# Block 1's rotary as two VectorE products and a TensorE sum, and its low weight parts kept off GpSimd

## The chip, the cores and the metric

One core of a Trainium2 chip runs the whole program in one launch. The metric is the device time of that program in microseconds (us); the kernel's figure is the median of three timed runs. Beside these there is one profiled execution, from which every row below comes. Engines carry their profile names: PE is TensorE's matmul, PEld its weight load, DVE is VectorE, ACT is ScalarE, POOL is GpSimd, SP is SyncE, which here issues most DMAs.

## The reference, cut to what matters

Two layers of a first block (gated delta rule, sparse attention with an indexer, mixture of experts) are followed by two layers of a second block. The change lies almost wholly in the first block's attention. There, five column groups of one projection are turned by rotary tables before they are used:

```python
def apply_rope(x, cos, sin):
    half = x.shape[-1] // 2
    rot = jnp.concatenate([-x[..., half:], x[..., :half]], -1)
    return x * cos + rot * sin          # per position and feature

proj = h @ w_in[l]                      # h: 272 x 1024, w_in: 1024 x 4176
q, k, qi, ki = (apply_rope(...) for the columns of sq, sk, iq, ik)
score = sum over 8 heads of relu(qi . ki / 8) * wi      # the indexer
sel   = top 64 keys of each query by score
out   = softmax(q . k / 8 over sel) @ v
```

The features lie in pairs 32 apart within each head of 64, and cos and sin are the same for both of a pair. In the second block the memory tokens are normed by rows (`rms_norm(mem, g)`) before a projection; one line of that is touched too.

## The kernel before, in words

Activations are held transposed, features on the 128 partitions and the 272 positions in the free dimension, as a high and a low part (`hh` and `hl`, L259 and L260). A weight tile of 1024 x 128 is split in the same way by `split`: ACT writes the high part `wh` (L244), and the low part `wl` (L245) is the difference, made on DVE, or on GpSimd for every fourth split, since `K.lo_pool` is 4 all through the first block. `ws` (L384) then multiplies: for each of 8 slices of 128 features three matmuls of 128x272 in the one-pass format (L252 high by high, L253 high by low, L254 low by high; the trace prints their type as f32), 24 in all, into one of three PSUM banks with the tag "d".

`rope` (L510) follows 13 such products in each of two layers: one for the indexer's keys `ikT`, four for its queries `iqT`, four for the keys `skT` and four for the queries `sqT`. It copies PSUM to `rraw` on ACT (L515, or L513 with the factor 0.125 for `sqT`), lets TensorE exchange the halves by a full float32 matmul against the constant `rot` (L517, into the single bank of tag "o"), multiplies `rraw` by cos on GpSimd (L519), the exchanged values by sin on DVE (L520), and adds both on GpSimd (L521).

The order on each engine is set at build time by a list scheduler, so a change of one engine's work moves its neighbours too. Around the first five ropes of a layer the delta rule still runs (L1151 to L1189: PE products of a state, sums on DVE, a power on GpSimd at L1178, which is followed by L1180 on DVE and the transposes L1183 on PE). Around the last eight the indexer runs: score products on PE (L543), relu on ACT (L546), weighted sums on DVE (L547), and eight rounds of maximum and replacement on DVE (L552, L553). After the ropes come the attention itself (L659 to L701), then the projection (`Project`, L252 to L254 again, with 512 columns), the norm (L788 to L865), routing, and the experts, whose weights (tiles `wb`, L1211) arrive through a ring of buffers.

`mem_kv` norms the memory rows in `memx`: a square on ACT (L1673), a power on GpSimd (L1675), and a product by a scalar for each row on DVE (L1676).

Of the kernel before, what the change touches and what calls it, by code (L numbers as in the profile page):

```python
# [8 lines left out]
F32 = mybir.dt.float32  # L9
# [4 lines left out]
OP = mybir.AluOpType  # L14
# [3 lines left out]
T1 = 272  # L18
# [355 lines left out]
def b1_attention(K, l, mix, st):  # L374
    nc, A, c = K.nc, K.A, K.c
    V, S, G, PE = nc.vector, nc.scalar, nc.gpsimd, nc.tensor
    p = K.p
    h2 = (K.hh, K.hl)
    w = A["w_in"][l]
    ident = c["ident"]  # L380
    tiles = (0, 1, 2) if l == 0 else (0, 1)

    def ws(wt, c0):
        wa = split(K, wt[:, :, c0:c0 + 128], (8, 128))  # L384
        ps = bank(K, "d")
        for k in range(8):
            mm3(K, ps[:, :T1], (wa[0][:, k], wa[1][:, k]), (h2[0][:, k, :], h2[1][:, k, :]), k == 0, k == 7)
        return ps[:, :T1]
# [118 lines left out]
    pa = K.pa = st["delta"].enter_context(K.tc.tile_pool(name="attr%d" % l, bufs=1, side="right"))  # L507


    def rope(ps, dst, scale=None):  # L510
        raw = p.tile([128, T1], F32, name="rraw", bufs=2)
        if scale:
            S.mul(raw, ps, scale)  # L513
        else:
            S.copy(raw, ps)  # L515
        pr = bank(K, "o")
        PE.matmul(pr[:, :T1], c["rot"], raw, start=True, stop=True)  # L517
        t2 = p.tile([128, T1], F32, name="rt2", tag="cva", bufs=2)
        G.tensor_tensor(dst, raw, c["cos"], op=OP.mult)  # L519
        V.tensor_tensor(t2, pr[:, :T1], c["sin"], op=OP.mult)  # L520
        G.tensor_tensor(dst, dst, t2, op=OP.add)  # L521

    K.router = router_weights(K, l, K.hp)
    ikT = p.tile([128, T1], F32, name="ikT", tag="ikT")
    rope(ws(wik.rearrange("p k a n -> p k (a n)"), 0), ikT)
# [33 lines left out]
    def heads():  # L559
        for x, o in ((skT, 2568), (sqT, 2056)):  # L560
            for b in range(2):
                wt = wcols(K, w, o + 256 * b)
                for j in range(2):

                    rope(ws(wt, j * 128), x[:, 2 * b + j, :], 0.125 if x is sqT else None)
                    yield
        for b in range(2):
            wt = wcols(K, w, 3080 + 256 * b)
            for j in range(2):
                ps = ws(wt, j * 128)  # L570
                raw = p.tile([128, T1], F32, name="rraw", bufs=2)
                S.copy(raw, ps)
                pt = bank(K)
                for t in range(3):
                    PE.transpose(pt[:TP[t], t * 128:(t + 1) * 128], raw[:, TOFF[t]:TOFF[t] + TP[t]], ident)
                ci = 2 * b + j
                for t in range(3):
                    S.copy(vtok[t][:TP[t], ci * 128:(ci + 1) * 128], pt[:TP[t], t * 128:(t + 1) * 128])
                yield
# [126 lines left out]
def router_weights(K, l, p):  # L706

    nc, A = K.nc, K.A
    V, S, G, PE = nc.vector, nc.scalar, nc.gpsimd, nc.tensor
    wr = K.pt.tile([128, 8, 36], F32, name="wr", tag="ta", bufs=2)  # L710
    nc.sync.dma_start(wr[:, :, 0:32], A["w_rtr"][l].rearrange("(k p) n -> p k n", p=128))
    nc.sync.dma_start(wr[:, :, 32:36], A["w_grp"][l].rearrange("(k p) n -> p k n", p=128))
    br = p.tile([36, 1], F32, name="br")
    nc.sync.dma_start(br[0:32], A["b_rtr"][l].rearrange("(n o) -> n o", o=1))
    nc.sync.dma_start(br[32:36], A["b_grp"][l].rearrange("(n o) -> n o", o=1))
    wrs = [p.tile([128, 8, 36], FR, name="wrs%d" % i) for i in range(2)]
    pr = bank(K, "o")
    for k in range(8):
        PE.matmul(pr[:36, 0:1], wr[:, k, :], K.lcol[:, 16 + 8 * l + k:17 + 8 * l + k], start=(k == 0), stop=(k == 7))
    with K.tc.issue_after(K.anchor.ins):  # L720
        V.tensor_tensor(br, br, pr[:36, 0:1], op=OP.add)
        V.tensor_tensor(wr, wr, K.lcol[:, 8 * l:8 * l + 8, None].to_broadcast([128, 8, 36]), op=OP.mult)
    put(K, wrs, wr, slice(None))
    return wrs, br
# [937 lines left out]
def mem_kv(K, l, pool):  # L1662

    nc, A = K.nc, K.A
    V, S, G, PE = nc.vector, nc.scalar, nc.gpsimd, nc.tensor
    mx = pool.tile([128, 2, 1024], F32, name="memx", tag="wb")
    nc.sync.dma_start(mx, A["mem_2"][0].rearrange("(t p) n -> p t n", p=128))
    yield
    mT = pool.tile([128, 8, 256], F32, name="memT", tag="wb")
    for t in range(2):  # L1670
        ss = K.pt.tile([128, 2], F32, name="rmss", bufs=2)
        sq = K.pt.tile([128, 1024], BF, name="rmsq", tag="ta", bufs=2)
        S.activation(sq, mx[:, t], AF.Square, accum_out=ss[:, 0:1])  # L1673
        V.tensor_scalar(ss[:, 0:1], ss[:, 0:1], 1.0 / 1024, 1e-6, op0=OP.mult, op1=OP.add)
        G.tensor_tensor(ss[:, 1:2], ss[:, 0:1], K.nhalf[:, 0:1], op=OP.pow)  # L1675
        V.tensor_scalar(mx[:, t], mx[:, t], ss[:, 1:2], None, op0=OP.mult)  # L1676
    g = K.lcol[:, 48 + 8 * l:56 + 8 * l]
    for b in range(4):
        ps = bank(K, "op"[b % 2])
        for kk in range(2):  # L1680
            for t in range(2):
                PE.transpose(ps[:, kk * 256 + t * 128:kk * 256 + t * 128 + 128],
                             mx[:, t, (2 * b + kk) * 128:(2 * b + kk + 1) * 128], K.c["ident"])
        V.tensor_tensor(mT[:, 2 * b:2 * b + 2, :], ps.rearrange("p (k q) -> p k q", k=2),
                        g[:, 2 * b:2 * b + 2, None].to_broadcast([128, 2, 256]), op=OP.mult)
    yield
    wv = A["mem_w_kv_2"][l].rearrange("(k p) n -> p k n", p=128)

    def proj(c0):
        ps = [bank(K, t) for t in "op"]  # L1690
        wt = []
        for b in range(2):
            wt.append(turn(K).rearrange("p (k n) -> p k n", n=512))
            nc.sync.dma_start(wt[b], wv[:, 4 * b:4 * b + 4, c0:c0 + 512])
        for b in range(2):
            for kk in range(4):
                k = 4 * b + kk
                for t in range(2):
                    PE.matmul(ps[t], mT[:, k, t * 128:(t + 1) * 128], wt[b][:, kk, :], start=(k == 0), stop=(k == 7))
            yield  # L1700
        return ps

    ps = yield from proj(0)
    if l == 1:
        m = pool.tile([128, 2048], F32, name="mkv", tag="wb")
        K.mem[1] = (m[:, 0:1024].rearrange("p (h q) -> p h q", q=256), m[:, 1024:].rearrange("p (t n) -> p t n", n=512))
    memk, memv = K.mem[l]
    kn = [mem_norm(K, x, 1.0) for x in ps]
    for t in range(2):
        S.mul(memk[:, :, t * 128:(t + 1) * 128], to_feat(K, kn[t], "op"[t]), K.lcol[:, 66 + l:67 + l])  # L1710
    yield
    ps = yield from proj(512)
    for t in range(2):
        S.copy(memv[:, t, :], ps[t])
    yield
# [638 lines left out]
```

## Time and profile before

| | |
|---|---|
| median of three runs | 2051.73 us (2047.42 to 2054.76) |
| the profiled execution, its own time | 2053.6 us |
| its span | 2051.8 us |
| PE busy | 1932.7 us, 94% of the span |
| DVE busy | 1057.3 us, 52% |
| ACT busy | 767.5 us, 37% |
| POOL busy | 353.9 us, 17% |
| GpSimd's low parts (L245) | 21 of 350, 50.4 us |
| the ropes of layer 0, of layer 1 | about 128 to 206 us, and 655 to 730 us |

A busy share is an average over stages. The rows that count are those of the two stretches in which the ropes lie; each row of a window gives the length, then for each engine the busy time and in brackets the number of instructions, then the granted share of TensorE's clock, the mean busy share of the DMA engines, and GB/s. A PE record's length holds the pipeline's depth, so back-to-back matmuls are read from start to start.

### The profile page before, as it was taken

The numbers are of one execution on the slowest core, as the hardware profiler recorded it, in microseconds if no ns is written. First come the engines' busy times: TensorE is split into PE (matmuls) and PEld (weight loads), VectorE is DVE, ScalarE is ACT, GpSimd is POOL, SyncE is SP. The second block draws the span as 40 slices with busy tenths as digits, with TensorE's granted clock in tenths as the row PEclk, the third lists the DMA queues.
The fourth block names the chain that finished last, engine by engine and source line by source line (L and its number), as shares of the span: only waits on it lengthen the run. The fifth ranks groups of instructions, "written<-read, shape, count | busy, mean of one in ns | idle before, by whom it ended". The sixth has DMA issues, their size and how long they took to land. (4 is left out here: it accounts for less than half of the span.)

```text
span 2051.8 us, 36697 instructions
## 1 busy us (share of the span) xinstructions
PE 1932.7 (94%) x15166; PEld 1523.2 (74%) x15166; DVE 1057.3 (52%) x2096; ACT 767.5 (37%) x1471; POOL 353.9 (17%) x370
## 2 busy tenths in 40 slices
PE   8999999999799998999779999999999999999999
PEld 7888755544588876544358698989888879898987
DVE  6557545222675664322165755555545675555544
ACT  4323432111341343211055344455435534445543
POOL 1325100000122620000010201224200030122410
PEclk9999989999899999999989999999999999999999
DMA  7313279999631346999973433445555353254551
GB/s 221 92 42 124 103 287 391 420 423 419 195 93 64 114 174 270 407 420 422 421 231 124 144 124 93 162 152 170 185 184 154 108 167 124 83 195 144 166 198 68
DMA packets 199341, 414.53 MB, mean 202 GB/s; under 512 B 26025, under 2 KB 147443, under 8 KB 174595
## 3 DMA queue, kind: packets, MB, share of 16 engines
q1 hardware_dynamic: 192230, 410.36, 55.1%
q10 hardware_dynamic: 6940, 1.78, 0.4%
q8 instruction: 121, 1.98, 0.4%
q14 instruction: 50, 0.40, 0.1%
HBM read 411.07 MB, written 1.05 MB: 201 GB/s over the span
## 5 line engine op out<-in xcount | busy, mean ns | idle before, releaser
L245 DVE TENSOR_TENSOR wl<-w,wh 128x1024 fp32r<-128x1024 f32 x329 | 412.9, 1257 | 263.3 <-ACT wh L244 260.0
L244 ACT CAST wh<-w 128x1024 fp32r<-128x1024 f32 x350 | 365.4, 1046 | 441.5 <-PE ps_d L253 266.5
L252 PE MATMUL ps_d<-hh,wh 128*128 128x256 f32 (+1 forms) x1632 | 485.7, 298 | 5.3 <-ACT wh L244 2.2
L254 PE MATMUL ps_d<-hh,wl 128*128 128x256 f32 (+1 forms) x1632 | 481.2, 295 | 0.2
L253 PE MATMUL ps_d<-hl,wh 128*128 128x256 f32 (+1 forms) x1632 | 478.7, 294 | 2.2 <-DVE hl L260 1.2
L252 PEld LDWEIGHTS ps_d<-hh,wh 128*128 128x128 f32 x1632 | 313.0, 192 | 17.4 <-issue 6.8
L254 PEld LDWEIGHTS ps_d<-hh,wl 128*128 128x128 f32 x1632 | 314.6, 193 | 10.3 <-DVE wl L245 6.8
L253 PEld LDWEIGHTS ps_d<-hl,wh 128*128 128x128 f32 x1632 | 313.9, 192 | 7.6 <-DVE hl L260 1.6
L1295 PE MATMUL ps_d<-wb,hg 128*32 128x256 f32 x1600 | 121.3, 388 | 6.0 <-DMA wb<-in_w 6.0
L2321 POOL TENSOR_TENSOR relu<-relu 128x256 f32<-128x256 f32 x64 | 86.7, 1354 | 130.6 <-ACT relu L2320 130.6
L1295 PEld LDWEIGHTS ps_d<-wb,hg 128*32 128x32 f32 x1600 | 59.3, 112 | 50.7 <-DMA wb<-in_w 10.5
L1327 DVE TENSOR_TENSOR yacc<-yacc,ps_c 128x512 f32<-128x512 f32 x56 | 38.5, 687 | 86.2 <-PE ps_c L1324 86.2
L1283 PE MATMUL ps_c<-oh,yp 128*128 128x128 f32 (+1 forms) x640 | 81.4, 280 | 0.0
L1283 PEld LDWEIGHTS ps_c<-oh,yp 128*128 128x128 f32 (+1 forms) x640 | 75.4, 191 | 7.9 <-issue 5.4
L1315 PE MATMUL ps_d<-wb,hid 128*32 128x512 f32 x400 | 70.5, 647 | 6.9 <-ACT hid L1309 6.8
L2275 POOL TENSOR_TENSOR mergedT<-mergedT,tg 128x256 f32<-128x256 f32 x32 | 32.6, 1040 | 239.4 <-DVE tg L2273 239.4
L245 POOL TENSOR_TENSOR wl<-w,wh 128x1024 fp32r<-128x1024 f32 x21 | 50.4, 2400 | 126.1 <-ACT wh L244 116.6
L1299 DVE SCALAR_TENSOR_TENSOR mth<-mth,ps_d 128x256 f32<-128x256 f32 x16 | 6.7, 421 | 125.2 <-ACT mth L1298 125.2
L1298 ACT ACTIVATE mth<-ps_d 128x256 f32<-128x256 f32 x16 | 6.1, 383 | 165.8 <-PE ps_d L1295 165.8
L1324 PE MATMUL ps_c<-ysl,ohT 128*128 128x512 f32 (+1 forms) x140 | 64.9, 603 | 0.0
L2322 ACT CAST hid<-relu 128x256 fp32r<-128x256 f32 x64 | 26.0, 407 | 92.3 <-POOL relu L2321 92.3
L2323 DVE TENSOR_TENSOR hid<-relu,hid 128x256 fp32r<-128x256 f32 x64 | 27.2, 425 | 58.5 <-ACT hid L2322 58.5
(697 smaller groups left out, 3578.0 us busy)
## 6 DMA issues: line engine op xcount, KB each, us to landing
wb<-in_w SPq DMA_DIRECT2D x150, 1024.0 KB, 14.3
w<-in_w_in SPq DMA_DIRECT2D x82, 1024.0 KB, 5.2
w<-in_w SPq DMA_DIRECT2D x42, 1024.0 KB, 19.6
w<-in_w_up SPq DMA_DIRECT2D x32, 1024.0 KB, 5.4
w<-in_w_down SPq DMA_DIRECT2D x32, 1024.0 KB, 5.0
w<-in_w_out SPq DMA_DIRECT2D x16, 1024.0 KB, 5.1
w<-in_w_branch SPq DMA_DIRECT2D x24, 512.0 KB, 3.6
w<-in_cmp_w SPq DMA_DIRECT2D x8, 1024.0 KB
```

What stands on the lines that cost most here:

```text
L244: K.nc.scalar.copy(h, x)
L245: eng.tensor_tensor(lo, x, h.bitcast(F32), op=OP.subtract)
L252: PE.matmul(out, a[0], b[0], start=start, stop=False, skip_group_check=True)
L253: PE.matmul(out, a[0], b[1], start=False, stop=False, skip_group_check=True)
L254: return PE.matmul(out, a[1], b[0], start=False, stop=stop, skip_group_check=True)
L1283: PE.matmul(ps[:, (k % 4) * 128:(k % 4) * 128 + 128], K.yp[t][:P, k * 128:(k + 1) * 128], oh[:P, t, :], start=(k == 4 * kk and t == ts[0] ...
L1295: PE.matmul(pu[j * 32:j * 32 + 32, i * 256:i * 256 + 256], hg[:, k, j * 32:j * 32 + 32], wts[i][j][:, k, :], start=(k == 0 and i == 0), st ...
L1315: PE.matmul(ps[q * 32:q * 32 + 32, :], hid[:, j, q * 32:q * 32 + 32], w2t[q][:, j, hf * 512:(hf + 1) * 512], start=(j == 0), stop=(j == 1) ...
L1324: PE.matmul(ps[rows[t]], ohT[:, off:off + P], ysl[:, hf * 512:(hf + 1) * 512], start=True, stop=True)
L1327: V.tensor_tensor(sl, sl, ps[rows[t]], op=OP.add)
L2275: G.tensor_tensor(m, m, tg, op=OP.add)
L2321: G.tensor_tensor(r, r, r, op=OP.mult)
```

## The change

Three things are edited.

- `rope`: DVE forms both products straight from the projection's PSUM bank (`rcos`, then `rsin`; the new L516), TensorE sums them in one bank by two float32 matmuls, one against the identity (L519) and one against `rot` (L520), and ACT writes the result with the scale in it (L521). The two scratch tiles keep their tags. That the exchange comes after the product by sin is allowed since sin is the same for both features of a pair. GpSimd has no part in it any more.
- `K.lo_pool` is 4 up to the definition of `rope` and 0 from there to the start of the next layer's attention. The splits of q, k, v and the gate still send every fourth low part to GpSimd; those of the ropes, of v and of the output projection don't. Of the 21 low parts on GpSimd 8 stay there.
- `mem_kv`: the product by row (now L1677) runs on ACT.

```diff
@@ b1_attention
     ident = c["ident"]
+    K.lo_pool = 4
     tiles = (0, 1, 2) if l == 0 else (0, 1)
...
-    def rope(ps, dst, scale=None):
-        raw = p.tile([128, T1], F32, name="rraw", bufs=2)
-        if scale:
-            S.mul(raw, ps, scale)
-        else:
-            S.copy(raw, ps)
+    def rope(ps, dst, scale=1.0):
+
+        parts = []
+        for nm, tag in (("cos", "rraw"), ("sin", "cva")):
+            x = p.tile([128, T1], F32, name="r" + nm, tag=tag, bufs=2)
+            V.tensor_tensor(x, ps, c[nm], op=OP.mult)
+            parts.append(x)
         pr = bank(K, "o")
-        PE.matmul(pr[:, :T1], c["rot"], raw, start=True, stop=True)
-        t2 = p.tile([128, T1], F32, name="rt2", tag="cva", bufs=2)
-        G.tensor_tensor(dst, raw, c["cos"], op=OP.mult)
-        V.tensor_tensor(t2, pr[:, :T1], c["sin"], op=OP.mult)
-        G.tensor_tensor(dst, dst, t2, op=OP.add)
-
+        PE.matmul(pr[:, :T1], ident, parts[0], start=True, stop=False)
+        PE.matmul(pr[:, :T1], c["rot"], parts[1], start=False, stop=True)
+        S.mul(dst, pr[:, :T1], scale)
+
+    K.lo_pool = 0
...
-                    rope(ws(wt, j * 128), x[:, 2 * b + j, :], 0.125 if x is sqT else None)
+                    rope(ws(wt, j * 128), x[:, 2 * b + j, :], 0.125 if x is sqT else 1.0)
@@ mem_kv
-        V.tensor_scalar(mx[:, t], mx[:, t], ss[:, 1:2], None, op0=OP.mult)
+        S.mul(mx[:, t], mx[:, t], ss[:, 1:2])
```

The scheduler moves rows with it. On PE, at the first `sqT` rope of layer 0 (`ps_d` is the projection's bank, `ps_o` the rope's, `cst_753` the table that holds `rot`), the kernel before has this:

```order
L254 MATMUL ps_d<-hh,wl 128x272
L543 MATMUL ps_c<-ikT,iqT 128x272 x2
L252 MATMUL ps_d<-hh,wh 128x272
L253 MATMUL ps_d<-hl,wh 128x272
L254 MATMUL ps_d<-hh,wl 128x272
L517 MATMUL ps_o<-rraw,cst_753 128x272
```

The same place on PE in the kernel after (`cst_94` holds the identity; L544 is the score product that was L543):

```order
L254 MATMUL ps_d<-hh,wl 128x272
L544 MATMUL ps_c<-ikT,iqT 128x272 x2
L519 MATMUL ps_o<-rcos,cst_94 128x272
L520 MATMUL ps_o<-rsin,cst_753 128x272
L252 MATMUL ps_d<-hh,wh 128x272
```

The rope's matmul stood three one-pass matmuls behind the scores; the two that take its place stand right behind them. At the `skT` ropes it is seven before and one after.

On DVE, where the indexer's first search meets the ropes in layer 0 (`m_2179` are the eight maxima), before:

```order
L552 MAX m_2179<-iacc 128x8
L553 MATCH_REPLACE iacc<-m_2179,iacc 128x144
L245 TENSOR_TENSOR wl<-w,wh 128x1024
L520 TENSOR_TENSOR rt_2175<-ps_o,cst_753 128x272
L552 MAX m_2179<-iacc 128x8
L547 SCALAR_TENSOR_TENSOR iacc<-irel,wis,cst_753 128x272
```

And after:

```order
L553 MAX m_2179<-iacc 128x8
L554 MATCH_REPLACE iacc<-m_2179,iacc 128x144
L516 TENSOR_TENSOR rcos<-ps_d,cst_753 128x272
L516 TENSOR_TENSOR rsin<-ps_d,cst_753 128x272
L553 MAX m_2179<-iacc 128x8
L245 TENSOR_TENSOR wl<-w,wh 128x1024
```

The two products now stand ahead of the low part, where the one product stood behind it.

On DVE in the delta rule of layer 0 (`uw_1421` and `state` are its running values), before:

```order
L1152 TENSOR_TENSOR uw_1421<-uw_1421,ps_c 64x512
L1164 TENSOR_TENSOR state<-state,ps_c 128x512
L245 TENSOR_TENSOR wl<-w,wh 128x1024
L1176 TENSOR_REDUCE dnst<-don 128x4
L520 TENSOR_TENSOR rt_1825<-ps_o,cst_753 128x272
```

And after, with the same instructions one line further down the file:

```order
L1153 TENSOR_TENSOR uw_1421<-uw_1421,ps_c 64x512
L516 TENSOR_TENSOR rcos<-ps_d,cst_753 128x272
L516 TENSOR_TENSOR rsin<-ps_d,cst_753 128x272
L245 TENSOR_TENSOR wl<-w,wh 128x1024
L1165 TENSOR_TENSOR state<-state,ps_c 128x512
L1177 TENSOR_REDUCE dnst<-don 128x4
```

Two products and a low part move ahead of a state's sum. On SP the load of the memory rows (L1667) moves ahead of one of the projection's weight loads (L219), in each layer.

## Rows read from the trace of the kernel before

**Rows 1.** The two stretches of the ropes and what follows each, by windows.
```profile
core 0: us, PE busy (x) PEld busy (x) DVE busy (x) ACT busy (x) POOL busy (x), PEclk, DMA share, GB/s
127.00:195.00 68.00, 64.43 (x475) 56.65 (x475) 40.29 (x75) 24.79 (x48) 34.88 (x34) 1.00 0.28 94
195.00:260.00 65.00, 64.72 (x437) 46.73 (x437) 39.48 (x85) 29.18 (x77) 15.69 (x24) 1.00 0.26 98
654.00:735.00 81.00, 79.17 (x583) 70.33 (x582) 53.33 (x103) 31.99 (x62) 43.04 (x39) 1.00 0.29 92
735.00:810.00 75.00, 68.07 (x413) 46.94 (x413) 35.45 (x100) 31.01 (x72) 9.41 (x21) 0.95 0.65 257
```

**Rows 2.** PE and its loads around one rope, in order of time (start, length, engine).
```profile
167.01 0.29 PE L253 MATMUL ps_d<-hl,wh 128*128 128x272 f32 x1
167.22 0.30 PEld L517 LDWEIGHTS ps_o<-rraw,cst 128*128 128x128 f32 x2
167.22 0.72 PE L517 MATMUL ps_o<-rraw,cst 128*128 128x272 f32 x2
167.56 0.19 PEld L254 LDWEIGHTS ps_d<-hh,wl 128*128 128x128 f32 x1
167.59 0.49 PE L254 MATMUL ps_d<-hh,wl 128*128 128x272 f32 x1
167.79 0.19 PEld L252 LDWEIGHTS ps_d<-hh,wh 128*128 128x128 f32 x1
167.91 0.29 PE L252 MATMUL ps_d<-hh,wh 128*128 128x272 f32 x1
...
168.04 0.29 PE L253 MATMUL ps_d<-hl,wh 128*128 128x272 f32 x1
```

**Rows 3.** The rope's matmul L517 by its source line: durations, then PE's idle time.
```profile
L517 PE MATMUL ps_o<-rraw,cst x52: 392/393/497, 129.2 to 727.2; 128*128 128x272 f32 x52
...
  ACT rraw L513: 2.4, 8
  ACT rraw L515: 1.8, 2
  issue: 0.5, 3
  ACT irel L546: 0.2, 1
```

**Rows 4.** The rope's DVE product L520, by its source line (min/median/max in ns).
```profile
L520 DVE TENSOR_TENSOR rt<-ps_o,cst x26: 420/428/441, 130.8 to 727.7; 128x272 f32<-128x272 f32 x26
```

**Rows 5.** One rope of the indexer's stretch, PE and then DVE, by the timeline.
```profile
201.11 0.28 PE L254 MATMUL ps_d<-hh,wl 128*128 128x272 f32 x1
201.32 0.73 PE L543 MATMUL ps_c<-ikT,iqT 64*128 64x272 f32 x4
201.98 0.39 PE L252 MATMUL ps_d<-hh,wh 128*128 128x272 f32 x1
...
202.34 0.29 PE L254 MATMUL ps_d<-hh,wl 128*128 128x272 f32 x1
202.70 0.72 PE L517 MATMUL ps_o<-rraw,cst 128*128 128x272 f32 x2
...
201.26 0.49 DVE L547 SCALAR_TENSOR_TENSOR iacc<-irel,wis,iacc 128x272 f32<-128x272 f32 x1
```

**Rows 6.** The low part L245 on DVE and on POOL, by its source line.
```profile
L245 DVE TENSOR_TENSOR wl<-w,wh x329: 1202/1225/2447, 14.9 to 2040.5; 128x1024 fp32r<-128x1024 f32 x165
L245 POOL TENSOR_TENSOR wl<-w,wh x21: 2347/2379/2692, 22.5 to 784.2; 128x1024 fp32r<-128x1024 f32 x21
```

**Rows 7.** PE's waits from 620 to 800 us (in total, times, longest), two lines of them.
```profile
PE ps_c L1183 <- DVE don L1180: 1.5, 2, 0.8
PE ps_d L253 <- POOL wl L245: 1.2, 1, 1.2
```

**Rows 8.** The delta rule's power on POOL and who waits, by the timeline of layer 0.
```profile
147.56 0.77 POOL L521 TENSOR_TENSOR iqT<-iqT,rt 128x272 f32<-128x272 f32 x1 [0.46 <-DVE dnst L1177]
148.29 1.03 POOL L1178 TENSOR_TENSOR dnst<-dnst,nhalf 128x4 f32<-128x4 f32 x1
...
150.19 0.63 PE L1183 MATMUL ps_c<-cst,don 128*128 128x128 f32 x4 [1.85 <-DVE don L1180]
```

**Rows 9.** DVE and POOL at the same time, by the timeline.
```profile
180.30 3.77 DVE L547 SCALAR_TENSOR_TENSOR iacc<-irel,wis,iacc 128x144 f32<-128x144 f32 x3
...
179.94 2.69 POOL L245 TENSOR_TENSOR wl<-w,wh 128x1024 fp32r<-128x1024 f32 x1 [0.64 <-ACT wh L244]
```

**Rows 10.** DVE near its limit, and the start of the experts, by windows of 10 us.
```profile
190.00:200.00 10.00, 9.85 (x68) 8.23 (x67) 9.83 (x24) 3.83 (x8) 4.55 (x4) 1.00 0.31 105
290.00:300.00 10.00, 10.00 (x23) 4.10 (x24) 3.10 (x16) 0.00 (x0) 0.00 (x0) 0.79 1.01 424
300.00:310.00 10.00, 10.00 (x130) 7.80 (x132) 3.65 (x27) 3.36 (x13) 0.00 (x0) 1.00 0.28 117
```

**Rows 11.** SP's longest wait before the experts' weights (in total, times, longest).
```profile
SPq L1211 <- PE ps_c L639: 41.8, 1, 41.8
```

**Rows 12.** ACT's and DVE's instructions that change places, by their source lines.
```profile
L513 ACT ACTIVATE rraw<-ps_d x8: 389/390/393, 188.2 to 726.4; 128x272 f32<-128x272 f32 x8
...
L515 ACT COPY rraw<-ps_d x18: 365/377/382, 128.0 to 708.3; 128x272 f32<-128x272 f32 x18
...
L1676 DVE TENSOR_SCALAR memx<-memx,rmss x4: 755/1004/1256, 175.3 to 702.7; 128x1024 f32<-128x1024 f32 x4
...
L244 ACT CAST wh<-w x350: 1027/1047/1056, 13.8 to 2039.4; 128x1024 fp32r<-128x1024 f32 x175
```

More of the change, by code (lines that the diff above doesn't have):

```diff
@@ L570, in heads @@
                 ps = ws(wt, j * 128)
-                raw = p.tile([128, T1], F32, name="rraw", bufs=2)
+                raw = p.tile([128, T1], F32, name="rraw", tag="rraw", bufs=2)
                 S.copy(raw, ps)
```

## The prediction

> **What bounds the kernel now.** I read the windows first, since a share over the whole span mixes stages. In the stretch of layer 0's ropes PE is busy 64.43 of 68 us, in what follows 64.72 of 65; in layer 1's it is 79.17 of 81, all at a granted clock of 1.00 (the 2.4 GHz level) [rows 1]. PE's starts bear this out: a one-pass matmul of 272 columns follows the last after 0.13 us (167.91 to 168.04) [rows 2]. So PE sets the pace here, and its idle time in the four windows, 3.57 + 0.28 + 1.83 + 6.93 = 12.6 us, is all that other engines could give back. DVE comes second: in the indexer's stretch it is busy 9.83 of 10 us [rows 10], though only 40.29 of 68 before it.
>
> Whether time gained or lost here reaches the end is read from the experts. SP holds their weights back 41.8 us until PE has done the attention's last product [rows 11]; then transfers run at 424 GB/s, and between 300 and 310 us they fall to 117 GB/s, while PE is busy throughout [rows 10]: the ring is full and waits for PE. The transfers start by PE's clock and wait for PE once more, so a delay before them shifts all that follows, one to one.
>
> **The change part by part.**
>
> *The added matmul.* Each of the 26 ropes gets one more float32 matmul of 272 columns (against the identity) in PE's queue. No row shows two such in a row, but the one there is can be taken apart. L517 is two records (x52 for 26 ropes) [rows 3]. A weight load starts when the matmul ahead of it begins to stream; the load for L254 starts at 167.56, the next at 167.79, so the second record streamed 0.23 us [rows 2]. A matmul right behind another needs two such passes, 0.46 us. The whole of L517 in its place cost more: from 167.14, where the next one-pass matmul would have started (167.01 + 0.13), to 167.91 - 0.13 = 167.78 (where the one behind it would have, had it not been queued) are 0.64 us, of which 0.08 is waiting for `rraw` (167.22 against 167.14) and the rest, 0.10, the first weight load, which nothing hid. So the added one costs between 0.46 and 0.64 us. I take 0.46, since its neighbour's load can run behind it, as the second record's did: 26 x 0.46 = **+12.0 us**, up to 26 x 0.64 = 16.6. PE is full, so all of it lies on the path, save what falls into idle time (below).
>
> *The wait for the rope's input.* PE waited 2.4 + 1.8 + 0.5 + 0.2 = 4.9 us in front of L517, mostly for ACT's copy [rows 3]. That copy goes; in its place PE waits for DVE's first product. Take the `sqT` rope at 201 us [rows 5]. The projection ends at 201.11 + 0.28 = 201.39, the scores leave PE at 201.98, and then three one-pass matmuls and a wait of 0.23 us (202.70 against 202.34 + 0.13) stood ahead of L517. The new pair stands right behind the scores. A product of 0.43 us [rows 4] started at once would end at 201.82, in time; but DVE was then in an indexer sum until 201.75 (201.26 + 0.49) [rows 5], and behind that the product ends at 202.18, 0.20 us late. That is the old wait in another place, so I take **0**. The bounds: all 4.9 us vanish where DVE is free; and where a low part of 1.23 us [rows 6] stands ahead with half its length on average, each rope waits some 0.4 us, 10.4 in all, +5.5.
>
> *Low parts off GpSimd.* 13 of 21 go to DVE, at 1.23 us each where GpSimd took 2.38 [rows 6]. PE waited for GpSimd's once in what changes, 1.2 us in layer 1's projection [rows 7]; DVE has done that part within the 1.2 us it saves. **-1.2 us**, and 0 at worst. The other twelve were ready before PE asked, and 12 x 1.23 us more on DVE costs nothing unless DVE becomes late (a rival).
>
> *The delta rule's neighbours.* Of the 1.85 us that PE waited for `don` in layer 0, GpSimd's addition ahead of the power L1178 made up 0.77 [rows 8]; that addition is gone. **-0.8 us**. At best all of this wait and the 1.5 us in layer 1 [rows 7] go, -3.4; at worst the two products and the low part that now stand ahead of a state's sum on DVE (2 x 0.43 + 1.23 = 2.1 us) [rows 4, 6] hold up PE's next product once a layer, less what PE has to do meanwhile: +2.
>
> *Edits with one answer.* ACT's 26 copies of 0.38 us become 26 scaled copies of 0.39, and ACT gets four passes over `memx` of about 1.05 us, by its nearest row, where DVE spent 1.0 [rows 12]; ACT is busy 24.79 of 68 us [rows 1], which hides them. If they hold up a high part that PE needs, 4.2 us. The memory rows' load moves ahead of one weight load on SP; the ring of four tiles hides that. Nothing waits for the rope's result sooner than before, since one ACT pass replaces two GpSimd ones.
>
> **Sum**: 12.0 + 0 - 1.2 - 0.8 = +10.0 us. On the profiled execution's own time, 2053.6, that is 2063.6 us. The median of the runs before is 2051.7, and their spread (2047.4 to 2054.8) holds 2053.6. I name 2063.
>
> **The rivals.**
>
> *GpSimd stood in DVE's way, and PE closes its gaps.* Three indexer sums took 3.77 us on DVE while GpSimd ran a low part of 2.69 us [rows 9]; two of another shape take 0.49 us each without one [rows 5]. With the low parts and the rope gone from GpSimd, such stretches end, DVE delivers everything before PE asks, and PE's idle time in the four windows goes: 12.0 - 12.6 = -0.6 us, **2053.0**, no slower than before. It decides if that idle time is caused by late DVE work. Against it: of the 12.6 us, 6.9 lie in layer 1's last window, where norm and routing end one after the other, and no line among PE's waits is on the indexer. The Trainium skill, "SBUF — State Buffer", in "Who interferes with whom", says that a VectorE instruction with two SBUF inputs and a GpSimd instruction that reads SBUF exclude each other for the whole instruction. The rows on the three sums agree; by that rule DVE gains, which is this rival, and PE gains only what it waited.
>
> *DVE becomes late.* DVE's work in the eight ropes of each indexer stretch grows by two products less one (8 x 0.43 = 3.4 us) and by two or three low parts (about 3 us), less 2 us of `memx`: some 4.5 us where it stood at 9.83 of 10 [rows 10]. If that queue runs late, the rope's products and the low parts behind them do, and PE with them: +4.5 us in each layer on top of the loads unhidden, 10.0 + 9 + 4.6 = +23.6, **2077**. Against it: what GpSimd stretched [rows 9] comes back, some us in each stretch. It decides if the low part that a projection needs stands behind the search.
>
> *The loss is hidden.* If the experts' weights were the bound from their first transfer, 12 us more before them would be covered and the time would be 2053.6 less 2, **2052**. The rows on SP and on the full ring speak against it.
>
> **How the numbers follow.** The forecast has a chance of 0.68, closed gaps 0.15, late DVE 0.13, hidden loss 0.04. The forecast's own range, by its bounds: 12.0 - 4.9 - 1.2 - 3.4 = +2.5 to 16.6 + 5.5 + 2 + 4.2 = +28.3; both ends need every bound at once, so I use half the way to each, +6 to +19, 2060 to 2073. To hold 8 in 10 the range reaches down to closed gaps and up into late DVE: **2053 to 2074**. A difference of 0.3% (6 us) is about what a measurement of this kernel can tell from none. Slower by more: 0.80 (most of the forecast, late DVE); within it: 0.16 (closed gaps for the most part, the hidden loss, the low end of the forecast); faster by more: 0.04.
>
> **What would show it.** In the changed profile: L519 and L520 with 52 records each at 0.39 us; starts of PE some 0.46 us further apart for each rope; PE's busy time up by 10 to 15 us in the rope's stretches; waits of PE for `rcos` of 3 to 6 us in all in place of those for `rraw`; no PE wait for GpSimd's `wl` in the projection; the first of the experts' products 4 to 6 us later in layer 0 and as much again in layer 1. The long indexer sums should be gone from DVE. I am wrong if the attention ends no later although PE does more (its idle time was DVE's making), or if waits for `rcos` or `wl` come to over 10 us.

## The result, and the profile after

The changed kernel takes 2062.97 us in the median (2056.29 to 2065.5, 11 runs); the kernel before, on the same chip, takes 2051.17 (2044.14 to 2054.76, 11 runs). The ratio is 1.0062, its 95% interval 1.0051 to 1.0073. It is slower by about 12 us, at the time that was named. The sum that led there was +10.0. One of its terms had the wrong sign, and smaller ones went the other way, as the rest of this document shows.

Lines of the changed kernel are one further on from L381. First its rope by source lines, as in [rows 3, 4, 12]: VectorE's two products, the identity matmul, the rotation matmul and ACT's scaled copy (min/median/max in ns, first and last start in us). The two rows without a line's name are PE's idle time in front of L519 alone. The last row is the indexer's sum.

```profile
L516 DVE TENSOR_TENSOR rcos<-ps_d,cst x26: 419/441/442, 128.7 to 739.4; 128x272 f32<-128x272 f32 x26
L516 DVE TENSOR_TENSOR rsin<-ps_d,cst x26: 422/430/432, 129.1 to 739.8; 128x272 f32<-128x272 f32 x26
L519 PE MATMUL ps_o<-rcos,cst x52: 392/394/497, 130.6 to 740.3; 128*128 128x272 f32 x52
...
  ACT wh L244: 1.4, 4
  DVE rcos L516: 0.5, 2
...
L520 PE MATMUL ps_o<-rsin,cst x52: 392/392/428, 131.1 to 740.8; 128*128 128x272 f32 x52
L521 ACT ACTIVATE sqT<-ps_o x8: 397/399/400, 193.1 to 741.2; 128x272 f32<-128x272 f32 x8
L548 DVE SCALAR_TENSOR_TENSOR iacc<-irel,wis,iacc x28: 361/426/503, 175.8 to 742.1; 128x144 f32<-128x144 f32 x14, 128x272 f32<-128x272 f32 x14
```

The identity matmul is there as two records for each of 26 ropes. VectorE's product takes 0.44 us. The list puts 0.5 us of PE's idle time down to it and 1.4 us to ACT's `wh`; the section on the prediction shows that the 1.4 us are waits for the product too. No sum of the indexer takes longer than 0.50 us, where three in [rows 9] took 3.77 together.

One rope of the changed kernel by the timeline, PE and then DVE; it answers to [rows 5]:

```profile
205.97 0.73 PE L544 MATMUL ps_c<-ikT,iqT 64*128 64x272 f32 x4
206.67 0.70 PE L519 MATMUL ps_o<-rcos,cst 128*128 128x272 f32 x2
207.20 0.62 PE L520 MATMUL ps_o<-rsin,cst 128*128 128x272 f32 x2
207.46 0.49 PE L252 MATMUL ps_d<-hh,wh 128*128 128x272 f32 x1
207.79 0.29 PE L253 MATMUL ps_d<-hl,wh 128*128 128x272 f32 x1
...
206.08 0.44 DVE L516 TENSOR_TENSOR rcos<-ps_d,cst 128x272 f32<-128x272 f32 x1 [1.57 <-PE ps_d L254]
206.44 0.43 DVE L516 TENSOR_TENSOR rsin<-ps_d,cst 128x272 f32<-128x272 f32 x1
```

From the rope's first matmul to the second one-pass matmul behind it are 207.79 - 206.67 = 1.12 us; in [rows 2] the same way, from 167.22 to 167.91, took 0.69. VectorE's product is done at 206.52 (206.08 + 0.44), and L519 starts 0.15 us behind it. From the scores' start to L519's are 0.70 us (205.97 to 206.67), where the matmul behind the scores in [rows 5] followed after 0.66 (201.32 to 201.98). So this rope waits for its product some 0.04 us, and the added matmul is nearly all that is paid.

To see where the 12 us lie, I cut both traces at the same work. Layer 0's ropes run from the first product of the delta rule's L1117 (L1118 after) to the first product of the attention's scores L659 (L660 after), and layer 1's likewise; these starts are the borders of the windows below. The experts' first products in layer 0 by source line, before (L1295) and after (L1296), and those of layer 1 after:

```profile
L1295 PE MATMUL ps_d<-wb,hg x403: 379/379/403, 305.6 to 419.9; 128*32 128x256 f32 x135
...
L1296 PE MATMUL ps_d<-wb,hg x330: 379/379/404, 310.2 to 399.9; 128*32 128x256 f32 x165
L1296 PE MATMUL ps_d<-wb,hg x528: 379/379/403, 828.6 to 949.7; 128*32 128x256 f32 x176
```

The windows of the ropes, first of the kernel before, then of the changed kernel:

```profile
127.80:217.30 89.50, 85.78 (x629) 75.77 (x628) 61.69 (x117) 34.43 (x72) 44.48 (x41) 1.00 0.32 111
656.10:741.50 85.40, 83.58 (x617) 74.36 (x615) 57.64 (x114) 33.96 (x69) 42.82 (x39) 1.00 0.31 99
```

```profile
129.30:222.10 92.80, 90.17 (x654) 80.23 (x652) 59.61 (x131) 37.53 (x73) 10.57 (x11) 1.00 0.32 109
664.30:755.40 91.10, 89.13 (x643) 79.01 (x641) 57.77 (x127) 37.33 (x72) 9.32 (x9) 1.00 0.29 94
```

The ropes take 3.3 us more in layer 0 and 5.7 in layer 1, 9.0 together, with PE's busy time up by 4.39 + 5.55 = 9.9 us. Between the two layers' ropes, where nothing of the rope runs, the way from the experts' first product to layer 1's ropes grew as well: 656.1 - 305.6 = 350.5 us before, 664.3 - 310.2 = 354.1 after. That is 3.6 us which the prediction has no term for. Layer 1's attention (from L659's first product to the first of the norm after it, L341) got 0.7 us shorter. Together 9.0 + 3.6 - 0.7 = 11.9 us. The two traces differ elsewhere as well, by +1.5 us ahead of layer 0's ropes and by -1.9 behind the start of layer 1's experts; two executions of one kernel differ by 2.9 and 2.2 us in these two places (the kernel with one low part back, below, whose first ropes start at 124.0 and at 126.9 us), so I read nothing from them.

PE's waits (in total, times, longest): first one of the kernel before, from 90 to 270 us, then those of the changed kernel from 90 to 270 and from 620 to 815 us, which answer to [rows 7]:

```profile
PE ps_c L1183 <- DVE don L1180: 2.1, 2, 1.9
...
PE ps_c L1184 <- DVE don L1181: 1.2, 2, 0.7
PE ps_o L519 <- DVE rcos L516: 0.4, 1, 0.4
...
PE ps_c L1015 <- POOL Tm L1071: 1.3, 3, 0.8
PE ps_c L1184 <- DVE don L1181: 1.1, 2, 0.6
PE ps_o L519 <- DVE rcos L516: 0.2, 1, 0.2
```

The wait for GpSimd's `wl` in the projection is gone. A wait for GpSimd's `Tm` (L1071) in layer 1's delta rule has grown; before, it was 0.4 us in two pieces.

### The profile page after: what moved, and what is told of

Same layout as the page of the kernel before. It is cut to its first block, busy times and chain, and to the rows that moved or that the text cites. A ratio compares the mean times of both kernels' runs of the same rounds, so it can differ in the third digit from the quotient of the medians.

```text
span 2063.5 us, 36707 instructions
## 1 busy us (share of the span) xinstructions
PE 1943.8 (94%) x15218; PEld 1534.4 (74%) x15218; DVE 1060.5 (51%) x2131; ACT 773.7 (37%) x1475; POOL 276.2 (13%) x305
## 3 DMA queue, kind: packets, MB, share of 16 engines
HBM read 411.07 MB, written 1.05 MB: 200 GB/s over the span
## 5 line engine op out<-in xcount | busy, mean ns | idle before, releaser
L245 DVE TENSOR_TENSOR wl<-w,wh 128x1024 fp32r<-128x1024 f32 x342 | 423.7, 1241 | 264.8 <-ACT wh L244 262.8
L252 PEld LDWEIGHTS ps_d<-hh,wh 128*128 128x128 f32 x1632 | 312.1, 192 | 14.1 <-issue 3.9
L1296 PE MATMUL ps_d<-wb,hg 128*32 128x256 f32 x1600 | 123.0, 391 | 6.4 <-DMA wb<-in_w 6.3
L1296 PEld LDWEIGHTS ps_d<-wb,hg 128*32 128x32 f32 x1600 | 59.9, 112 | 51.7 <-DMA wb<-in_w 10.3
L252 PE MATMUL ps_d<-o,wh 128*128 128x256 f32 x192 | 55.2, 287 | 0.0
```

What stands on the lines that cost most here:

```text
L245: eng.tensor_tensor(lo, x, h.bitcast(F32), op=OP.subtract)
L252: PE.matmul(out, a[0], b[0], start=start, stop=False, skip_group_check=True)
L1296: PE.matmul(pu[j * 32:j * 32 + 32, i * 256:i * 256 + 256], hg[:, k, j * 32:j * 32 + 32], wts[i][j][:, k, :], start=(k == 0 and i == 0), st ...
```

## The experiments

This table has what each kernel's rows of those products and windows give: the length of the ropes' stretch in each layer, and PE's busy time in it (us). The medians and ratios (to the kernel before on the same chip) stand at each experiment.

| kernel | layer 0, length | PE busy | layer 1, length | PE busy |
|---|---|---|---|---|
| before | 89.5 | 85.78 | 85.4 | 83.58 |
| changed | 92.8 | 90.17 | 91.1 | 89.13 |
| new rope alone | 94.5 | 90.42 | 97.5 | 90.83 |
| all but the rope | 87.9 | 85.02 | 87.0 | 84.04 |
| no identity matmul | 86.1 | 84.10 | 85.2 | 83.40 |
| two identity matmuls | 100.4 | 96.35 | 97.6 | 95.31 |
| VectorE's sum | 85.8 | 83.97 | 85.0 | 83.42 |
| ACT's exchange | 81.7 | 78.56 | 80.9 | 77.37 |

### One part of the change at a time

The first kernel has the new rope, with low parts and memory rows as before:

```diff
-    K.lo_pool = 0
     K.router = router_weights(K, l, K.hp)
...
-        S.mul(mx[:, t], mx[:, t], ss[:, 1:2])
+        V.tensor_scalar(mx[:, t], mx[:, t], ss[:, 1:2], None, op0=OP.mult)
```

> The changed rope alone: every fourth low part stays on GpSimd and the memory rows' product on VectorE, as before. Theory A (the 26 added TensorE passes are the loss, 26 x 0.46 = 12 us, less waits of 1 to 3 us that the shorter wait for the product saves): 9 to 12 us over the kernel before, 2060 to 2063. Theory B (a part of the loss comes from the low parts and the memory rows, which crowd VectorE and ScalarE): 4 to 8 us over before, 2055 to 2059.

It took 2065.65 us (5 runs), ratio 1.0087 (1.0072 to 1.0103): both theories were too low. The rope alone costs no less than the whole change; whether it costs more can't be told, since the whole change was 1.0062 (1.0051 to 1.0073) and in a second set 1.0077 (1.0063 to 1.0090). The ropes' stretches themselves are 8.1 us longer than the changed kernel's by the table. The rows of this trace, which is of the fastest of the five runs, say why: the first two are of L519 by source line, with the idle time in front of it, the others one wait by the timeline, on GpSimd, DVE and PE.

```profile
L519 PE MATMUL ps_o<-rcos,cst x52: 392/394/497, 127.4 to 738.4; 128*128 128x272 f32 x52
...
  DVE rcos L516: 6.6, 5
...
700.10 2.85 POOL L245 TENSOR_TENSOR wl<-w,wh 128x1024 fp32r<-128x1024 f32 x1 [0.19 <-ACT wh L244]
...
700.61 2.50 DVE L547 SCALAR_TENSOR_TENSOR iacc<-irel,wis,cst 128x144 f32<-128x144 f32 x1
...
704.32 0.75 DVE L1676 TENSOR_SCALAR memx<-memx,rmss 128x1024 f32<-128x1024 f32 x1 [0.67 <-POOL rmss L1675]
704.99 0.43 DVE L516 TENSOR_TENSOR rcos<-ps_d,cst 128x272 f32<-128x272 f32 x1
...
705.57 0.70 PE L519 MATMUL ps_o<-rcos,cst 128*128 128x272 f32 x2 [2.24 <-DVE rcos L516]
```

PE waits 6.6 us for `rcos`, where the changed kernel waits 1.9 (0.5 and 1.4, above). The longest piece, 2.24 us, is a rope's product that stands on DVE behind two things: an indexer sum of 2.50 us beside a low part on GpSimd (no sum of the changed kernel takes over 0.50), and the scaling of the memory rows, which itself waits for GpSimd's power. The change takes that low part off GpSimd and puts that scaling on ACT. So the parts belong together: with the products on DVE, whatever waits on DVE makes PE wait.

The second kernel has everything but the rope:

```diff
+    K.lo_pool = 4
...
     def rope(ps, dst, scale=None):
...
+    K.lo_pool = 0
     K.router = router_weights(K, l, K.hp)
...
-        V.tensor_scalar(mx[:, t], mx[:, t], ss[:, 1:2], None, op0=OP.mult)
+        S.mul(mx[:, t], mx[:, t], ss[:, 1:2])
```

> The change without its rope: the low parts of the ropes' products and of the output projection all on VectorE, the memory rows' product on ScalarE, the rope as before. Theory A: 1 to 3 us faster than before (the wait of 1.2 us for GpSimd's low part in layer 1's projection goes, and some of GpSimd's queue ahead of the delta rule's power), 2048 to 2050. Theory B: 3 to 6 us slower than before, 2054 to 2057.

2049.75 us (12 runs), ratio 1.0004 (0.9992 to 1.0016): no difference that can be measured, so neither theory A's gain nor theory B's loss. Its ropes are 1.6 us shorter in layer 0 and 1.6 longer in layer 1; the way from layer 0's experts to layer 1's ropes, 350.5 us before, is 354.4 here, as long as in the changed kernel.

### The identity matmul: none, and two

The first of these two kernels leaves the product by cos out of the sum, the second adds it twice.

```diff
-        PE.matmul(pr[:, :T1], ident, parts[0], start=True, stop=False)
-        PE.matmul(pr[:, :T1], c["rot"], parts[1], start=False, stop=True)
+        PE.matmul(pr[:, :T1], c["rot"], parts[1], start=True, stop=True)
```

> The changed kernel without the identity matmul: the product by cos is still made on VectorE but left out of the sum, so the rope's result lacks that part. Theory A: the matmul lies on the path with its whole length, so 26 x 0.46 = 12 us come off the changed kernel: 2051, within 2 us of before, and a little under it where the earlier start of the rope pays. Rival (TensorE waits for VectorE's second product in the time that the identity matmul filled, 0.2 to 0.3 us a rope): only 4 to 7 us come off, 2056 to 2059.

2049.84 us (12 runs), ratio 1.0003 (0.9988 to 1.0018): all of the loss is gone, 13.1 us from the changed kernel's median. By the table the ropes are 6.7 + 5.9 = 12.6 us shorter than the changed kernel's, and PE is busy 6.07 + 5.73 = 11.8 us less. Against the kernel before they are 3.4 us shorter in layer 0 and 0.2 in layer 1.

```diff
         PE.matmul(pr[:, :T1], ident, parts[0], start=True, stop=False)
+        PE.matmul(pr[:, :T1], ident, parts[0], start=False, stop=False)
```

> The changed kernel with the identity matmul written twice in each rope (the cosine part is counted twice in the sum). Theory A, the added pass lies on a full TensorE at the price that the changed kernel's records show (229 ns a record, two records): 26 x 0.458 = +11.9 us on the changed kernel's 2063.0, about 2075 (2073 to 2077), and the starts of a rope's records at 0, 304, 533, 762, 991, 1220 ns. Theory B, part of an added pass falls into time that TensorE would have waited for VectorE's products or for weights (the four windows of the changed kernel leave TensorE 9.9 us idle): +4 to +8 us, 2067 to 2071.

2077.53 us (4 runs), ratio 1.0130 (1.0110 to 1.0151): theory A, half a microsecond above its range. One rope by the timeline, PE, and the waits in front of L519:

```profile
179.78 0.70 PE L519 MATMUL ps_o<-rcos,cst 128*128 128x272 f32 x2
180.32 0.62 PE L520 MATMUL ps_o<-rcos,cst 128*128 128x272 f32 x2
180.78 0.62 PE L521 MATMUL ps_o<-rsin,cst 128*128 128x272 f32 x2
181.03 0.49 PE L253 MATMUL ps_d<-hl,wh 128*128 128x272 f32 x1
181.36 0.29 PE L254 MATMUL ps_d<-hh,wl 128*128 128x272 f32 x1
...
  DVE rcos L516: 2.9, 5
```

A matmul between two others takes 180.78 - 180.32 = 0.46 us, and the whole way is 181.36 - 179.78 = 1.58, 0.46 more than with one. The stretches grew by 7.6 + 6.5 = 14.1 us, 11.9 of it the matmuls. Of the rest, 1.0 us is PE's idle time in front of L519, up from 1.9 to 2.9 us; some 1.2 us stay open.

### One low part ahead of layer 1's ropes

The prediction has no term for the 3.6 us ahead of layer 1's ropes. In the kernel before, one low part runs on GpSimd at 617.54 us, in layer 1's delta rule; it is that of `ikT`, split early. The change puts it on DVE. This kernel moves one line of the changed kernel, so that only this low part goes back:

```diff
-    K.lo_pool = 0
     K.router = router_weights(K, l, K.hp)
     ikT = p.tile([128, T1], F32, name="ikT", tag="ikT")
     rope(ws(wik.rearrange("p k a n -> p k (a n)"), 0), ikT)
+    K.lo_pool = 0
```

> The changed kernel with one low part fewer moved: the first rope's (for ikT) stays under the old rule, which puts that of layer 1 back on GpSimd, in front of the delta rule's L1071. In the kernel before it ran there at 617.54 us (2.36 us on GpSimd); in the changed kernel VectorE makes it, the mask products that GpSimd's Tm (L1071) waits for come later, TensorE waits 1.3 us in three pieces for Tm instead of 0.4 in two, and a stretch of 7 us behind it runs at a granted clock of 0.66 instead of 1.00. The time from the end of layer 0's experts to the first rope of layer 1 was 124 to 126 us in the profiles of all six kernels without that low part on GpSimd that were looked at, and 120 to 121 in the three with it. Theory A, this low part is the cause: 3 to 4 us come back, the stretch is 120 to 121 us again, 2059 to 2060. Theory B, the clock's dip there has another cause or comes by chance: no difference, 2062 to 2064.

2058.2 us (6 runs), ratio 1.0048 (1.0030 to 1.0066), a little under theory A's range. Since that was on another chip than the changed kernel's runs, both ran once more, side by side.

> The changed kernel as it is, on one chip beside the kernel with one low part back on GpSimd, since those two had been timed on different chips. Both theories: 2061 to 2065. Its profile has TensorE waits of about 1.3 us for Tm (L1071) between 600 and 660 us and a granted clock near 0.66 in the 7 us behind.

> The changed kernel with the first rope's low part of layer 1 back on GpSimd, beside the changed kernel on one chip. Theory A, this low part costs what the profiles show: 3 to 5 us under the changed kernel beside it. Theory B, what the profiles show there evens out over executions (the kernel with VectorE's sum gained nothing by the same edit in its median): within 2 us of the changed kernel beside it.

The changed kernel took 2063.61 us (2062.51 to 2065.44, 5 runs), ratio 1.0077 (1.0063 to 1.0090); with the low part back it was 2057.67 us (2056.7 to 2059.8, 5 runs), ratio 1.0047 (1.0033 to 1.0061). Theory A holds: 5.9 us, more than its 3 to 5, and the two sets of runs do not overlap. The expectation was off in how it comes about. Here is the changed kernel in that run: GpSimd's `Tm` between 620 and 630 us by source line, DVE's low part and PE's wait by the timeline, and two windows behind.

```profile
L1071 POOL TENSOR_TENSOR Tm<-cst,Z x5: 309/822/1632, 622.0 to 626.9; 64x256 f32<-64x256 f32 x4, 16x64 f32<-16x64 f32 x1
...
624.08 1.22 DVE L245 TENSOR_TENSOR wl<-w,wh 128x1024 fp32r<-128x1024 f32 x1
...
625.94 0.68 PE L1015 MATMUL ps_c<-cst,Tm 64*64 64x64 f32 x14 [0.81 <-POOL Tm L1071]
...
625.00:632.00 7.00, 5.74 (x94) 4.79 (x95) 2.60 (x7) 0.74 (x2) 2.42 (x3) 0.73 0.48 150
632.00:639.00 7.00, 7.00 (x131) 6.30 (x130) 3.21 (x8) 1.34 (x2) 0.00 (x0) 0.78 0.02 5
```

The same views with the low part back on GpSimd:

```profile
620.12 2.36 POOL L245 TENSOR_TENSOR wl<-w,wh 128x1024 fp32r<-128x1024 f32 x1
...
L1071 POOL TENSOR_TENSOR Tm<-cst,Z x5: 307/730/866, 622.4 to 625.7; 64x256 f32<-64x256 f32 x4, 16x64 f32<-16x64 f32 x1
...
625.00:632.00 7.00, 6.57 (x162) 5.64 (x158) 2.25 (x9) 0.74 (x2) 1.31 (x2) 1.00 0.76 265
632.00:639.00 7.00, 7.00 (x145) 6.26 (x142) 4.62 (x13) 1.34 (x2) 0.00 (x0) 1.00 0.01 2
```

DVE's operations ahead of `Tm` come no later. One of GpSimd's subtractions takes 1632 ns where the longest is otherwise 866, and DVE's low part of 1.22 us lies beside it. PE, which waits for `Tm`, loses 0.8 us more in 625 to 632 us (busy 5.74 against 6.57). Then its granted clock falls: 0.73 and 0.78 in two windows, where the other kernel has 1.00, so that part of them ran at the lower of the two levels (1.2 GHz). In the trace of the changed kernel taken first, the same place has 1.3 us of waits and 0.66 in the second window. The loss of a clock level costs (0.27 + 0.22) x 7 = 3.4 us of full-speed time, four times the wait that came ahead of it. The way from layer 0's experts to layer 1's ropes is 3.5 us longer (354.1 against 350.6). These traces are of the middle runs, and of the 5.9 us between them 2.2 lie behind the start of layer 1's experts and 0.7 ahead of layer 0's ropes, where both kernels do the same; so 3.5 us are shown to be the low part's, and the rest is not.

The other traces agree. With this low part on DVE, in eight traces (the changed kernel twice, the second to the sixth of the table's variants, and the one with the memory rows' evacuation on ACT, below), the long subtraction takes 1627 to 1632 ns and the granted clock falls behind it, to between 0.55 and 0.76 in the 7 us that follow. With it on GpSimd, in six (the kernel before among them), no subtraction takes over 868 ns and the clock there stays at 1.00. The way from layer 0's experts to layer 1's ropes is 354.0 to 360.2 us in the eight and 349.4 to 350.6 in five of the six; in the sixth (ACT's exchange with every fourth low part back, below) it is 354.3, for a reason that is open.

### Ropes with less work for TensorE

The identity matmul does on TensorE a sum that DVE could do. This rope has two DVE products with the scale in them, one matmul, and a sum on DVE:

```diff
-            V.tensor_tensor(x, ps, c[nm], op=OP.mult)
+            V.scalar_tensor_tensor(x, ps, scale, c[nm], op0=OP.mult, op1=OP.mult)
...
-        PE.matmul(pr[:, :T1], ident, parts[0], start=True, stop=False)
-        PE.matmul(pr[:, :T1], c["rot"], parts[1], start=False, stop=True)
-        S.mul(dst, pr[:, :T1], scale)
+        PE.matmul(pr[:, :T1], c["rot"], parts[1], start=True, stop=True)
+        V.tensor_tensor(dst, pr[:, :T1], parts[0], op=OP.add)
```

> The changed kernel with the sum on VectorE instead of TensorE: the identity matmul goes, VectorE adds the exchanged values out of PSUM to the product by cos (0.43 us a rope, 26 of them), the factor for the queries is taken into the products, and ScalarE has no part in the rope. Theory A (TensorE bounds, VectorE has room since GpSimd no longer holds it up): 11 to 14 us under the changed kernel, 2049 to 2052. Rival (VectorE becomes late in the indexer's stretch by 8 x 0.43 = 3.4 us a layer): 5 to 8 us under it, 2055 to 2058.

2046.52 us (12 runs), ratio 0.9991 (0.9977 to 1.0004): 16 us under the changed kernel, below the ranges of both theories, and not to be told from the kernel before. The ropes are 7.0 and 6.1 us shorter than the changed kernel's.

The next one takes the rotation matmul away too. ACT exchanges the blocks of 32 rows out of PSUM:

```diff
...
+        for b in range(4):
+            o = 32 * b
+            S.mul(x[o:o + 32, :], ps[o ^ 32:(o ^ 32) + 32, :], scale if b % 2 else -scale)
+        V.tensor_tensor(x, x, c["sin"], op=OP.mult)
+        V.tensor_tensor(dst, cs, x, op=OP.add)
```

> The kernel with VectorE's sum, whose remaining rotation matmul goes too: ACT exchanges the 32-row blocks with four copies of 32 rows out of PSUM, signed, VectorE multiplies by cosine out of PSUM and by sine out of SBUF and adds; TensorE has no work in the rope. Theory A, TensorE's own work is what the rope costs: from 2046.5 go 26 x 0.46 to 26 x 0.64 us, 12.0 to 16.6, so 2030 to 2035, and the starts of the rope stretches' matmuls are 0.13 us apart throughout. Theory B, ACT becomes late: 104 copies of about 0.38 us are 40 us more on ACT in the rope stretches, the high parts of the weights stand behind them, and TensorE waits for those: 2040 to 2052, with waits of TensorE for ACT's wh (L244) above 5 us.

2046.01 us (12 runs), ratio 0.9990 (0.9974 to 1.0006). The ropes are 4.1 us shorter in each layer than with VectorE's sum, but the time is the same. That lies in theory B's range, though its sign, long waits for `wh`, is absent: the attention behind the ropes, from L659's first product to the first of the norm after it (L341), grew by 2.2 us in layer 0 and 3.7 in layer 1. ACT's copies by source line, and two of PE's waits between 640 and 800 us:

```profile
L518 ACT ACTIVATE rsin<-ps_d x104: 387/389/394, 127.1 to 724.2; 32x272 f32<-32x272 f32 x104
...
PE ps_o L1682 <- DVE memT L1684: 1.1, 1, 1.1
PE ps_c L575 <- ACT rraw L572: 0.8, 1, 0.8
```

Behind the ropes appear waits that the trace of VectorE's sum does not have: for DVE's evacuation of the memory rows (`memT`) and for ACT's copy of a value head. Two edits went for one engine each. The first put that evacuation on ACT, the second gave GpSimd its low parts back:

```diff
-        V.tensor_tensor(mT[:, 2 * b:2 * b + 2, :], ps.rearrange("p (k q) -> p k q", k=2),
-                        g[:, 2 * b:2 * b + 2, None].to_broadcast([128, 2, 256]), op=OP.mult)
+        for kk in range(2):
+            S.mul(mT[:, 2 * b + kk, :], ps[:, kk * 256:kk * 256 + 256], g[:, 2 * b + kk:2 * b + kk + 1])
```

> The kernel with ACT's exchange, and the scaling of the transposed memory rows (four VectorE operations of 0.68 us a layer, L1684, which stood behind the indexer's search) on ACT as eight of 256 columns. In the kernel with ACT's exchange TensorE's busy time in the ropes and the attention fell by 4.3 and 3.4 us a layer against the one with VectorE's sum, but its idle time rose by 2.4 and 3.1. Theory A, the remaining bound is VectorE's search and what stands behind it: the waits of 1.1 us for memT go and VectorE ends earlier by 2.7 us a layer, -2 to -4 us, 2042 to 2044. Theory B, ACT is the late engine: the eight added operations (3 us a layer) hold up its copies for the value heads, 0 to +3, 2046 to 2049.

```diff
-    K.lo_pool = 0
     K.router = router_weights(K, l, K.hp)
```

> The kernel with ACT's exchange, and every fourth low part of a weight back on GpSimd in the rope's stretch, as before. Theory A, VectorE's time bounds: a low part of 1.24 us less for each one that moves, -2 to -4 us, 2042 to 2044. Theory B, GpSimd's slower low parts (2.4 us) and their company with VectorE cost more than they relieve, as they did with the changed rope alone: 0 to +4, 2046 to 2050, with waits of TensorE for GpSimd's wl of 1 us and more.

They took 2048.05 us, ratio 1.0005 (0.9992 to 1.0019), and 2044.12 us, ratio 0.9989 (0.9976 to 1.0002), 12 runs each. The first lies in theory B's range, the second at the edge of A's; neither can be told from the kernel before. In the first one's trace the attention takes 57.4 and 50.6 us, 0.6 us from that with VectorE's sum, so the edit does end the growth behind the ropes; that the median shows nothing of it, and which engine bounds this rope, stays open. Last, VectorE's sum with the one low part of layer 1 back on GpSimd, the edit that gained 5.9 us above:

> The kernel with VectorE's sum and the same one low part of layer 1 back on GpSimd. Theory A, the low part is the cause of the slow stretch ahead of layer 1's ropes: 3 to 4 us under the kernel with VectorE's sum (2046.5), 2042 to 2044, which is 0.2 to 0.3% under the kernel before. Theory B, no difference: 2046 to 2048.

2048.24 us (12 runs), ratio 0.9994 (0.9980 to 1.0008): theory B, no gain in the median, although the wait for `Tm` is 0.4 us again in its trace and 0.8 with VectorE's sum alone, whose trace also has the fall of the clock. That trace is of its slowest run (2055.68 us), so it may not stand for the middle one. Why the same edit gains nothing here is open. None of the kernels beats the one before beyond what can be measured.

## Why the prediction was right, and where it was wrong

- *The added matmul, +12.0.* Right, and at the end that was taken. The timeline shows 0.46 us for each (180.32 to 180.78), which is 26 x 0.46 = 12.0; PE's busy time shows 11.8, the stretches without it 12.6. The upper bound of 0.64 held the first weight load, which nothing hid; in the row of three the first matmul takes 0.54 us (179.78 to 180.32) and the next 0.46.
- *The wait for the rope's input, 0.* Right in size, though the lists hide it. The 4.9 us of [rows 3] add PE and its weight loads; of PE alone one wait of 0.8 us is listed (the last fence of this section). But a PE record is longer than its time on the engine, so shorter waits show only from start to start: the eight `sqT` ropes waited 0.23 to 0.24 us each ([rows 5]: 202.70 against 202.34 + 0.13), 1.9 in all, and with the 0.8 that is about 2.7 us. In the changed kernel the list names 0.5 us for `rcos` and 1.4 us, at four `sqT` ropes, for `wh`. Those are waits for `rcos` too: in the rows below this list `rcos` ends at 196.93, L519 starts 0.15 us later, as in the rope at 206 us, and its weight load starts at 197.05, before the cast of `wh` ends at 197.06. On DVE a round of the indexer's search (L554) stood ahead of `rcos`. From the scores' start this L519 comes after 1.05 us, against 0.66 in [rows 5]: 0.39 us of waiting. Read like this, four of the eight `sqT` ropes wait 0.4 to 0.5 us and four 0.04, 1.9 in all again, and with the 0.5 that is about 2.4 us. So this term is about -0.3, and the 3 to 6 us foreseen for `rcos` were a little too many. The sum on DVE that made the product late in [rows 5] is not what does it; the search is.
- *Low parts off GpSimd, -1.2, and 0 at worst.* Wrong in sign. The wait of 1.2 us in the projection is gone, and layer 1's attention is 0.7 us shorter, but the low part ahead of layer 1's ropes costs 3.6 us in the trace and, side by side, 5.9 in the medians. The step that failed is "12 x 1.23 us more on DVE costs nothing unless DVE becomes late": DVE is not late, it stands in GpSimd's way. The rival of GpSimd in DVE's way named that contact, and the sum did not ask for its other direction. The Trainium skill, "SBUF — State Buffer", in "Who interferes with whom", says that whichever of the two engines issues first blocks the other. The subtraction of 1632 ns, which began some 0.2 us behind the low part, agrees with it.
- *The delta rule's neighbours, -0.8.* Right. The waits for `don` fell from 2.1 to 1.2 us in layer 0 and from 1.5 to 1.1 in layer 1, -1.3.
- *ACT's copies and `memx`, 0.* As said, with a gain that was not seen: the rope alone shows that `memx` left on DVE helps to hold up a product, and PE with it.
- *Reaching the end.* The experts' first product starts 4.6 us later in layer 0, as foreseen, and 13.6 later in layer 1, 9.0 more instead of "as much again", mostly by the 3.6 us above.
- *What the sum has no term for.* In the ropes 12.0 - 0.3 - 1.3 = 10.4 us should show, and 9.0 do. Some 0.9 us of the difference can be read in [rows 5]: behind the scores two one-pass matmuls took 0.36 us (201.98 to 202.34), where two take 0.25 elsewhere, and at the eight `sqT` ropes of the changed kernel no such pair follows the scores. The other 0.5 us are open.

A `sqT` rope of the changed kernel by the timeline, and PE's idle time in front of L517 in the kernel before, that of PE alone (us, times):

```profile
196.02 1.04 ACT L244 CAST wh<-w 128x1024 fp32r<-128x1024 f32 x1 [2.48 <-PE ps_d L253]
196.03 0.73 PE L544 MATMUL ps_c<-ikT,iqT 64*128 64x272 f32 x4
...
196.29 0.29 DVE L554 MATCH_REPLACE8 iacc<-m,iacc 128x144 f32<-128x144 f32 x1
196.50 0.43 DVE L516 TENSOR_TENSOR rcos<-ps_d,cst 128x272 f32<-128x272 f32 x1
...
197.05 0.30 PEld L519 LDWEIGHTS ps_o<-rcos,cst 128*128 128x128 f32 x2 [0.71 <-issue]
...
197.08 0.70 PE L519 MATMUL ps_o<-rcos,cst 128*128 128x272 f32 x2 [0.32 <-ACT wh L244]
...
  ACT rraw L515: 0.8, 1
```

By rows the terms are +12.0 - 0.3 - 1.3 - 0.9 - 0.7 + 3.6 = +12.4, against +11.9 in the stretches and 11.8 in the medians. The forecast of +10.0 had the largest term to a few per cent and the rope's input about right; the low parts were some 4 us too cheap, and three smaller gains together 1.7 us too small. That the time named was met is in part luck: +10.0 was added to the profiled execution's 2053.6 us, which lies 2.4 us above the median of 2051.17, and this made up for the 1.8 us that the sum lacked.

The rivals: "DVE becomes late" came about only at the four ropes behind the search, 0.4 to 0.5 us each, and not as a queue that runs late. "PE closes its gaps" had its cause right, since the long indexer sums went, but PE gave back only about 4 us and not 12.6. The hidden loss did not occur.

## What to carry to other kernels

Where TensorE is busy throughout a stretch, price a matmul added to it by the spacing of starts in the trace, times its count, and believe it; a sum over two operands belongs there only if no other engine has time for it. Before work moves from GpSimd to VectorE, look at what both run at that moment in every place, also in stages that are not part of the edit: a short wait there can cost TensorE its clock level, and that costs more than the wait. Read idle time by engine, since a group that holds a matmul and its weight load counts both; and check TensorE's waits from start to start, since the list leaves out short ones and can name an engine that merely finished at the same moment.

## What the runs showed of the hardware

- GpSimd's subtraction of 64x256 took 1627 to 1632 ns beside a VectorE low part of 1.22 us in eight traces, and at most 868 ns without one in six.
- A granted clock of 0.73 and 0.78 in two windows of 7 us, 3.4 us of full-speed time, followed 0.8 us of extra waiting; without that wait the same place stayed at 1.00.
- ACT's copy of 32 partitions x 272 took 389 ns, that of 128 x 272 took 399 ns: four copies of 32 rows cost four times one of 128.
